# Sending more transposes of a two-layer hybrid encoder through transposing transfers

## The chip, the cores and the metric

The kernel runs on one core of a Trainium2 chip. A core has engines that each work through their own instructions in order: TensorE (PE, with its weight load PEld), VectorE (DVE), ScalarE (ACT), GpSimd (POOL) and SyncE (SP), which here issues almost all transfers (DMA). They wait for one another through semaphores. The metric is the device time of one execution in microseconds (us).

## The reference

Two layers over 256 tokens of 1024 channels, one sequence. What the change touches, cut to its core:

```python
u = rms_norm(h, g_mix_pre)
(gq, gk, gv, gg, ra_f, ra_b, aq, ak, av, gate_a, gate_b) = jnp.split(u @ w_in, offsets, axis=-1)
...
o_gla = rms_norm(o_f + o_b, g_gla_out)             # gated linear attention, two directions
branch_a = (o_gla * jax.nn.silu(gg)) @ w_o_gla     # the gated output
q = apply_axial_rope(rms_norm(aq, g_q_norm), cos, sin)
branch_b = gqa_attention(q, k, v) @ w_o_attn       # 8 query heads, 2 groups of 4
mixed = sigmoid(gate_a) * branch_a + sigmoid(gate_b) * branch_b
h = h + rms_norm(mixed @ w_out, g_mix_post)
```

Then a SwiGLU FFN with 2816 hidden channels and a per-layer embedding follow, each with norms and a residual add. All is f32.

## The kernel before

**Products.** Each f32 operand is split into a high part (a cast to the fp32r type) and a low part (value minus high part). A product is three matmuls, high by high, high by low and low by high, of 128 x 128 stationary activations and 512 columns of weights. Since the contraction runs over partitions, activations are needed transposed: channels on partitions, tokens free.

**Weights.** Every weight comes once from HBM in units of 1 MB on SP's queue, into one of two `raw` tiles. ACT casts a unit to `wh` in two pieces of 128 x 1024, DVE subtracts it to `wl` in two (`split`, L134), and PE uses it. Both kinds have four tiles each, so a cast can begin only when PE has given an older unit back (`done`). For gate B and three pairs of FFN blocks (2, 6, 8) a seven-product scheme is used: there some raw units are borrowed ("lent") from the `wh` and `wl` tiles or from a big tile, and DVE adds and combines units of 128 x 2048 between the casts.

**Order.** PE's work stands in program order: the long products are written out, and smaller jobs (transposes, attention, gla) are `Task` generators that go on at ticks, two to each group of twelve matmuls. The numbers a task yields (`W`, `WAIT_MIX`, `WAIT_TURNED` = 9 and others) are ticks that it lets pass. The framework orders the other engines' instructions by priority; `tc.high_priority(AHEAD)` puts instructions forward and `tc.issue_after(x)` puts them behind `x` on the same engine.

**Two ways of transposing.** `transpose_in` has PE transpose four 128 x 128 blocks into PSUM (L449, the queries' at L1267); ACT casts the result out of PSUM and DVE subtracts. `turn_out` and `take_in` use a transfer instead: ACT copies the f32 words into two planes of 16 bits (L463 or L468), SP issues a DMA transpose of the two planes (L469), and later ACT joins the planes to f32 words again (L476), casts, and DVE subtracts. Before, only the FFN's hidden blocks go that way, nine a layer, each with a fresh `mid` tile; the last pair's go through PE.

**The places.** `out_gate` (stage `gg`, PE's part in stage `gate`) multiplies gla output and SiLU of the gate and has PE transpose the product, sixteen blocks a layer (`turn_in(gT, sg, hf, W["g"])`). `attend(g)` transposes the queries of four heads for each half of the tokens (`hf`), takes the softmax, transposes it, and multiplies by the values. `merge(1)` adds the two gated branches and has PE transpose the sum in blocks (j, hf) for the out projection. `turned` in the FFN sends a hidden block out and takes it in.

## Time and profile before

| what | value |
|---|---|
| median of 3 runs | 909.61 us (909.36 to 910.53) |
| profiled execution | 909.68 us |
| its span | 907.9 us |
| granted TensorE clock | 0.999 |
| PE, PEld, DVE, ACT, POOL busy | 99%, 84%, 87%, 68%, 12% |
| moved by DMA | 178.16 MB, 196 GB/s on the mean |

The profile is of one execution; about 1.8 us of its time lie around the span. A row of the timeline gives the start, the time, the engine, the line of the kernel, the operation, the tiles written and read, and the count; idle time ahead of it and what ended it stand in brackets. A tile's name has its stage: `0gate` is the gate stage of layer 0, `1ffnin` the FFN of layer 1, `at` attention, `gla` linear attention, `gg` the gla output gate. Matmuls overlap, so one is best priced by the distance of starts and not by its duration.

### The profile page before, as it was taken

How to read it: one execution, taken by the hardware profiler on the slowest of the kernel's cores; microseconds unless marked ns; L12 is line 12 of the kernel's file. 1: busy time of each engine (PE TensorE's matmuls, PEld its weight loads, DVE VectorE, ACT ScalarE, POOL GpSimd, SP SyncE). 2: the span in 40 equal slices, each digit the busy share in tenths (PEclk: the TensorE clock that was granted, in tenths of full speed). 3: DMA queues.
4: the chain of work that ended last, by engine and by line, in shares of the span. 5: the costliest groups of instructions: out<-in, count | busy, mean ns of one | idle time of the engine just before them, and what ended most of it. 6: DMA issues, size and time to landing. Idle time of an engine off the chain costs nothing.

```text
span 907.9 us, 12157 instructions
## 1 busy us (share of the span) xinstructions
PE 898.8 (99%) x4479; PEld 762.2 (84%) x4479; DVE 790.2 (87%) x1021; ACT 620.5 (68%) x1011; POOL 105.9 (12%) x157
## 2 busy tenths in 40 slices
PE   9999999999999999999999999999999999999997
PEld 8898888888888887887898888888888888888886
DVE  7999989987668999998779899799876799999984
ACT  7688677564467787756676687675644796958563
POOL 3700221300100000000254001110000000000001
PEclk9999999999999999999999999999999999999999
DMA  8663445657397594956576424455573966858461
GB/s 283 219 189 136 140 140 191 216 187 249 115 288 204 173 301 146 317 170 233 180 279 204 168 93 140 139 186 185 186 241 100 309 180 206 254 210 264 150 231 47
DMA packets 108519, 178.16 MB, mean 196 GB/s; under 512 B 22494, under 2 KB 46566, under 8 KB 107948
## 3 DMA queue, kind: packets, MB, share of 16 engines
q1 hardware_dynamic: 108300, 177.25, 59.9%
q8 instruction: 35, 0.57, 0.3%
q14 instruction: 24, 0.20, 0.1%
q10 hardware_dynamic: 160, 0.14, 0.0%
HBM read 169.50 MB, written 3.15 MB: 190 GB/s over the span
## 4 chain that ended last, share of the span: by engine, by line
PE 78%; DVE 11%; DMA 4%; issue 4%; ACT 2%; POOL 0%; SPq 0%; POOLq 0%; ACTq 0%; DVEq 0%
PE acc_1ffnin L122 12%; PE acc_0gate L122 7%; PE acc_1gate L122 7%; PE acc_1ffnin L106 7%; DVE wl_0ffnin L134 6%; PE acc_1rq L122 3%; PE acc_0gqk L106 2%; PE acc_1gqk L106 2%; PE acc_1wout L122 2%; PE acc_0ple L122 2%; PE acc_1v L122 2%; PE acc_0gg L122 2%; PE acc_1gg L122 2%; PE acc_0v L122 2%; PE acc_0merge L122 2%
## 5 line engine op out<-in xcount | busy, mean ns | idle before, releaser
L134 ACT CAST wh_0ffnin<-raw_0ffnin 128x1024 fp32r<-128x1024 f32 x38 | 38.1, 1048 | 19.8 <-DMA raw_0ffnin<-in_w_ffn_out_dram 10.2
L134 ACT CAST wh_1ffnin<-raw_1ffnin 128x1024 fp32r<-128x1024 f32 x38 | 38.3, 1048 | 17.4 <-DMA raw_1ffnin<-in_w_ffn_out_dram 5.0
L134 DVE TENSOR_TENSOR wl_0ffnin<-raw_0ffnin,wh_0ffnin 128x1024 fp32r<-128x1024 f32 x38 | 44.6, 1219 | 5.8 <-ACT wh_0ffnin L134 5.8
L134 DVE TENSOR_TENSOR wl_1ffnin<-raw_1ffnin,wh_1ffnin 128x1024 fp32r<-128x1024 f32 x38 | 44.8, 1219 | 5.0 <-ACT wh_1ffnin L134 4.9
L106 PE MATMUL acc_0ffnin<-wh_0ffnin,big_0ffnin 128*128 128x512 f32 x176 | 45.4, 392 | 0.0
L106 PE MATMUL acc_1ffnin<-wh_1ffnin,big_1ffnin 128*128 128x512 f32 x176 | 45.1, 390 | 0.0
L122 PE MATMUL acc_0ffnin<-wh_0ffnin,big_0wout 128*128 128x512 f32 x168 | 41.8, 390 | 0.0
L122 PE MATMUL acc_1ffnin<-wh_1ffnin,big_1wout 128*128 128x512 f32 x168 | 41.5, 389 | 0.0
L106 PEld LDWEIGHTS acc_0ffnin<-wh_0ffnin,big_0ffnin 128*128 128x128 f32 x176 | 32.8, 188 | 7.5 <-DVE big_0ffnin L134 0.5
L106 PEld LDWEIGHTS acc_1ffnin<-wh_1ffnin,big_1ffnin 128*128 128x128 f32 x176 | 33.0, 188 | 6.9
L122 PEld LDWEIGHTS acc_0ffnin<-wh_0ffnin,big_0wout 128*128 128x128 f32 x168 | 31.4, 188 | 7.1 <-ACT wh_0ffnin L134 0.4
L122 PEld LDWEIGHTS acc_1ffnin<-wh_1ffnin,big_1wout 128*128 128x128 f32 x168 | 31.5, 188 | 6.5
L134 DVE TENSOR_TENSOR wl_1ffnin<-lent_1ffnin,wh_1ffnin 128x1024 fp32r<-128x1024 f32 x30 | 35.7, 1217 | 0.6 <-ACT wh_1ffnin L134 0.6
L134 DVE TENSOR_TENSOR wl_0ffnin<-lent_0ffnin,wh_0ffnin 128x1024 fp32r<-128x1024 f32 x30 | 35.6, 1216 | 0.1
L134 ACT CAST wh_1ffnin<-lent_1ffnin 128x1024 fp32r<-128x1024 f32 x30 | 30.7, 1051 | 5.4 <-PE acc_1ffnin L106 3.9
L134 ACT CAST wh_0ffnin<-lent_0ffnin 128x1024 fp32r<-128x1024 f32 x30 | 30.4, 1053 | 3.6 <-DVE lent_0ffnin L332 3.4
L134 ACT CAST wh_0gate<-raw_0gate 128x1024 fp32r<-128x1024 f32 x20 | 19.9, 1049 | 14.4 <-DMA raw_0gate<-in_w_o_attn_dram 6.1
L134 ACT CAST wh_1gate<-raw_1gate 128x1024 fp32r<-128x1024 f32 x20 | 19.9, 1048 | 13.9 <-PE acc_1gate L122 5.9
L134 DVE TENSOR_TENSOR wl_0gate<-raw_0gate,wh_0gate 128x1024 fp32r<-128x1024 f32 x20 | 24.2, 1257 | 5.2 <-ACT wh_0gate L134 5.1
L134 DVE TENSOR_TENSOR wl_1gate<-raw_1gate,wh_1gate 128x1024 fp32r<-128x1024 f32 x20 | 23.5, 1221 | 5.1 <-ACT wh_1gate L134 5.1
L106 PE MATMUL acc_0ffnin<-wl_0ffnin,big_0ffnin 128*128 128x512 f32 x88 | 24.6, 394 | 0.6 <-DVE wl_0ffnin L134 0.6
L106 PE MATMUL acc_1ffnin<-wl_1ffnin,big_1ffnin 128*128 128x512 f32 x88 | 24.0, 391 | 0.0
(730 smaller groups left out, 2731.7 us busy)
## 6 DMA issues: line engine op xcount, KB each, us to landing
raw_0ffnin<-in_w_ffn_out_dram SPq DMA_DIRECT2D x11, 1024.0 KB, 5.9
raw_1ffnin<-in_w_ffn_out_dram SPq DMA_DIRECT2D x11, 1024.0 KB, 5.5
lent_0ffnin<-in_w_ffn_in_dram SPq DMA_DIRECT2D x6, 1024.0 KB
lent_1ffnin<-in_w_ffn_in_dram SPq DMA_DIRECT2D x6, 1024.0 KB, 7.5
raw_0v<-in_w_in_dram SPq DMA_DIRECT2D x4, 1024.0 KB, 5.8
raw_0gate<-in_w_o_gla_dram SPq DMA_DIRECT2D x4, 1024.0 KB, 6.8
raw_0gate<-in_w_o_attn_dram SPq DMA_DIRECT2D x4, 1024.0 KB, 5.2
raw_0wout<-in_w_ffn_in_dram SPq DMA_DIRECT2D x8, 512.0 KB, 4.6
```

Source lines behind the costliest of these rows:

```text
L106: return nc.tensor.matmul(o, lhsT, rhs, start=start, stop=stop)
L122: nc.tensor.matmul(o, x, y, start=start and n == 0, stop=stop and n == len(seq) - 1, **kw)
L134: return nc.scalar.copy(hi, src), nc.vector.tensor_tensor(out=lo, in0=src, in1=hi.bitcast(F32), op=ALU.subtract)
```

## The change

- Gated output: no PE transposes. Each half tile of 512 channels of `sg` is sent out by `turn_out`, in place: its planes go to the part of `gg` that has been used, the transpose comes back into `sg`. It is taken in after 9 ticks (hf = 0) or 11 (hf = 1), the second half tile a tick later. Four transfers a layer in place of sixteen transposes.
- Queries of g = 1: sent out after the last exponential of g = 0, with the planes over g = 0's half of the same tile, and taken in where PE transposed before. Two transfers a layer in place of eight transposes.
- Mix: the one block with j < hf, that is j = 0 and hf = 1, is sent out when it is made and taken in after 9 ticks, behind the last addition of the merge. One transfer a layer in place of four transposes.
- FFN: the transpose now comes back into the hidden block's own tile and the join goes to the planes' tile, so a `mid` tile serves two blocks.
- Queue order: the stream notes its last load (SP) and last weight cast (ACT and DVE). A transfer is issued behind that load, and a join with its cast and subtraction behind that weight cast (`turn`).

In all 56 PE transposes go; 14 transfers come, each with a split and a join on ACT. PE's order is otherwise the same but for a few matmuls that change places around the second group's scores. DVE has the same kinds of subtraction.

```diff
@@ -28,9 +28,10 @@
 WAIT_NEXT, WAIT_IN, WAIT_H = (7, 9), ((6, 9), (6, 6)), ((3, 5), (3, 5))
-WAIT_MIX = 3, 6
+WAIT_MIX = 3, 6, 9
 WAIT_SPREAD = 12
-W = dict(r=5, z=6, s0=4, s=3, s1=9, o0=1, o=1, k=4, q=3, a0=1, a1=4, a2=4, a3=1, g=6)
+W = dict(r=5, z=6, s0=4, s=3, s1=9, o0=1, o=1, k=4, q=3, a0=1, a1=4, a2=4, a3=1)
+WAIT_GATED = 9, 11
 
@@ -256,6 +257,7 @@
             self.loads, self.jobs, self.lend, self.last = [], [], False, {}
+            self.queue = {}
             pairs = {}
@@ -294,7 +296,9 @@
                     if self.open:
-                        nc.sync.dma_start(dst, src)
+                        load = nc.sync.dma_start(dst, src)
+                        if not x.own:
+                            self.queue["SP"] = load
                     else:
@@ -317,7 +321,7 @@
             for piece in self.put(x):
-                split(*piece)
+                self.queue["ACT"], self.queue["DVE"] = split(*piece)
 
@@ -348,9 +352,16 @@
                 for piece in pieces or ():
-                    self.last[n] = split(*piece)
+                    self.last[n] = self.queue["ACT"], self.queue["DVE"] = split(*piece)
                 if pieces:
                     self.load()
+
+        def turn(self, *engines):
+            stack = ExitStack()
+            for e in engines:
+                if e in self.queue:
+                    stack.enter_context(tc.issue_after(self.queue[e].ins))
+            return stack
 
@@ -452,32 +463,29 @@
 
-    def turn_out(src, k, hf):
+    def turn_out(src, parts, mixed=False):
 
         with tc.high_priority(AHEAD):
-            both, turned = halves(mid())
-            turned = turned.bitcast(U16)
-            parts = both.bitcast(U16).rearrange("p (s c) -> p s c", s=2)
-            words = src.bitcast(U16)
-            if hf is None:
+            planes, words = (t.bitcast(U16) for t in (parts, src))
+            if mixed:
                 nc.scalar.copy(
-                    parts.rearrange("p s (k h f) -> p s k h f", k=2, f=P),
+                    planes.rearrange("p (s k h f) -> p s k h f", s=2, k=2, f=P),
                     words.rearrange("p (h k f s) -> p s k h f", h=2, f=P, s=2),
                 )
             else:
-                nc.scalar.copy(parts, words.rearrange("p (c s) -> p s c", s=2))
-            nc.sync.dma_start_transpose(out=turned.rearrange("p (x t) -> p x t", t=P), in_=parts.rearrange("p s c -> p (s c)"))
-        return both, turned
-
-    def take_in(sp, both, turned, k, hf):
-
-        n, tn = (2, T) if hf is None else (4, P)
-        hi, lo = sp.at(k, n, (hf or 0) * P, tn)
-        nc.scalar.copy(
-            both.bitcast(U16).rearrange("p (k t s) -> p k t s", s=2, t=tn),
-            turned.rearrange("p (s k t) -> p k t s", s=2, t=tn),
-        )
-        split(hi, lo, both.rearrange("p (k t) -> p k t", t=tn))
+                nc.scalar.copy(planes.rearrange("p (s c) -> p s c", s=2), words.rearrange("p (c s) -> p s c", s=2))
+        with ws.turn("SP"):
+            nc.sync.dma_start_transpose(out=words.rearrange("p (x t) -> p x t", t=P), in_=planes)
+
+    def take_in(hi, lo, src, parts):
+
+        tn = hi.shape[-1]
+        with ws.turn("ACT", "DVE"):
+            nc.scalar.copy(
+                parts.bitcast(U16).rearrange("p (k t s) -> p k t s", s=2, t=tn),
+                src.bitcast(U16).rearrange("p (s k t) -> p k t s", s=2, t=tn),
+            )
+            split(hi, lo, parts.rearrange("p (k t) -> p k t", t=tn))
 
@@ -1261,12 +1269,14 @@
                 yield W["q"]
-                ps = aux()
-                for i in range(4):
-                    hd = 4 * g + i
-                    nc.tensor.transpose(ps[:, i * P : (i + 1) * P], qrs[hf][:, hd * P : (hd + 1) * P], ident)
                 qh, ql = halves(mid(F32R))
-                split(qh, ql, ps)
+                if g == 0:
+                    ps = aux()
+                    for i in range(4):
+                        nc.tensor.transpose(ps[:, i * P : (i + 1) * P], qrs[hf][:, i * P : (i + 1) * P], ident)
+                    split(qh, ql, ps)
+                else:
+                    take_in(*(t.rearrange("p (i t) -> p i t", t=P) for t in (qh, ql)), *halves(qrs[hf])[::-1])
                 qs.append((qh, ql, qss[hf][:, 4 * g : 4 * g + 4]))
@@ -1274,6 +1284,10 @@
                 yield W["a1"]
+            if g == 0:
+                for qr in qrs:
+                    with tc.issue_after(last_exp[0].ins):
+                        turn_out(*halves(qr)[::-1])
             for hf in range(2):
@@ -1459,7 +1473,16 @@
                     vmul(t, t, on[:, hf, s])
-                turn_in(gT, sg, hf, W["g"])
+                xs = [(t, gg[:, hf, j * 512 : (j + 1) * 512]) for j, t in enumerate(halves(sg))]
+                for x in xs:
+                    turn_out(*x)
+
+                def turn(hf=hf, xs=xs):
+                    for j, x in enumerate(xs):
+                        yield WAIT_GATED[hf] if j == 0 else 1
+                        take_in(*gT.at(4 * j, 4, hf * P, P), *x)
+
+                gT.makers[hf].append(Task(turn(), part[0]))
 
@@ -1512,16 +1535,24 @@
 
+        mixed = []
+
         def merge(br):
             def then(j, hf, o):
                 sl = [s[:, hf, j * 512 : (j + 1) * 512] for s in sgate[: br + 1]]
                 vmul(sl[br], o, sl[br])
                 if br == 1:
-                    nc.vector.tensor_tensor(out=sl[0], in0=sl[0], in1=sl[1], op=ALU.add)
+                    mixed.append(nc.vector.tensor_tensor(out=sl[0], in0=sl[0], in1=sl[1], op=ALU.add))
 
                     def turn():
-                        yield WAIT_MIX[hf]
-                        transpose_in(mixT, sl[0], 4 * j, 4, hf)
+                        if j < hf:
+                            turn_out(*sl)
+                        yield WAIT_MIX[2 if j < hf else hf]
+                        if j < hf:
+                            with tc.issue_after(mixed[-1].ins):
+                                take_in(*mixT.at(4 * j, 4, hf * P, P), *sl)
+                        else:
+                            transpose_in(mixT, sl[0], 4 * j, 4, hf)
 
@@ -1567,7 +1598,7 @@
         part[0] = f"{l}ffnin"
-        hid = Split()
+        hid, spare = Split(), []
         us = [[ws.take() for _ in range(2)] for _ in range(2)]
@@ -1577,9 +1608,12 @@
                 else:
-                    x = turn_out(src, k, hf)
+                    if not spare:
+                        spare.extend(halves(mid()))
+                    parts = spare.pop()
+                    turn_out(src, parts, hf is None)
                     yield WAIT_TURNED
-                    take_in(hid, *x, k, hf)
+                    take_in(*(hid.at(k, 2, 0, T) if hf is None else hid.at(k, 4, hf * P, P)), src, parts)
 
```

How it moves ACT in the gate stage of layer 0, before (`lent`, `raw` and a big tile hold weights; `aux_0gg` is PE's transpose in PSUM):

```order
L134 CAST wh_0gate_1680<-lent_0gate_1670 128x1024 x2
L134 CAST wh_0gate_1747<-raw_0gate_1676 128x1024 x2
L134 CAST big_0gg_1719<-aux_0gg_1714 128x4x128
L134 CAST big_0gg_1727<-aux_0gg_1722 128x4x128
L134 CAST big_0gg_1719<-aux_0gg_1730 128x4x128
L134 CAST big_0gg_1727<-aux_0gg_1737 128x4x128
L1475 ACTIVATE big_0gate_1744<-acc_0gate_1598,rs_start_120 128x512
L1475 ACTIVATE big_0gate_1744<-acc_0gate_1599,rs_start_121 128x512
L134 CAST wh_0gate_1781<-big_0gate_1672 128x1024 x2
L134 CAST wh_0gate_1805<-raw_0gate_1678 128x1024
L740 COPY mid_0gate_1788<-acc_0gate_1790 128x512
```

and after:

```order
L476 COPY big_0gg_1272<-mid_0gg_1632 128x1024 x2
L135 CAST wh_0gate_1684<-lent_0gate_1674 128x1024
L476 COPY big_0gg_1272<-mid_0gg_1642 128x1024 x2
L135 CAST wh_0gate_1684<-lent_0gate_1674 128x1024
L1498 ACTIVATE big_0gate_1718<-acc_0gate_1594,rs_start_120 128x512
L1498 ACTIVATE big_0gate_1718<-acc_0gate_1595,rs_start_121 128x512
L135 CAST wh_0gate_1721<-raw_0gate_1680 128x1024 x2
L484 COPY big_0gg_1272<-mid_0gg_1632 128x1024 x2
L135 CAST big_0gg_1749<-big_0gg_1272 128x4x128
L135 CAST big_0gg_1759<-big_0gg_1272 128x4x128
L135 CAST wh_0gate_1763<-big_0gate_1676 128x1024 x2
L484 COPY big_0gg_1272<-mid_0gg_1642 128x1024 x2
```

Four casts out of PSUM stood together behind the casts of two units. Now four splits (L476, two to a row) surround the first unit's pieces, and the joins (L484, two to a row) with their casts stand between the next units' casts; the second pair's casts follow.

ACT at the splits of the second group's queries in layer 0, before (`mx`, `sm` belong to the softmax of g = 0, `aux_0at` is its transpose):

```order
L1237 ACTIVATE mid_0at_811,sm_0at_822<-aux_0at_812,mx_0at_819,qss_0rq_164 128x256 x2
L1302 ACTIVATE big_0gqk_639<-acc_0gqk_783 128x256
L1237 ACTIVATE mid_0at_811,sm_0at_838<-aux_0at_828,mx_0at_835,qss_0rq_164 128x256 x2
L134 CAST wh_0gqk_911<-raw_0gqk_773 128x1024
L134 CAST mid_0at_892<-aux_0at_887 128x512
L134 CAST mid_0at_900<-aux_0at_895 128x512
L134 CAST wh_0gqk_911<-raw_0gqk_773 128x1024
```

and after:

```order
L1245 ACTIVATE mid_0at_811,sm_0at_822<-aux_0at_812,mx_0at_819,qss_0rq_164 128x256 x2
L1316 ACTIVATE big_0gqk_639<-acc_0gqk_783 128x256
L1245 ACTIVATE mid_0at_811,sm_0at_838<-aux_0at_828,mx_0at_835,qss_0rq_164 128x256 x2
L476 COPY mid_0rq_161<-mid_0rq_161 128x1024
L476 COPY mid_0rq_163<-mid_0rq_163 128x1024
L135 CAST mid_0at_896<-aux_0at_891 128x512
L135 CAST mid_0at_904<-aux_0at_899 128x512
L135 CAST wh_0gqk_915<-raw_0gqk_773 128x1024 x2
```

Two copies have come in behind the last exponential, ahead of the casts of the transposed softmax and of weights.

ACT at the first hidden blocks of the FFN in layer 0, before (L1596 is the SiLU, L468 the split, L476 the join):

```order
L1596 ACTIVATE t_0ffnin_2594<-acc_0ffnin_2622 128x256
L453 COPY mid_0wout_2298<-aux_0wout_2643 128x512
L468 COPY mid_0ffnin_2665<-t_0ffnin_2594 128x1024
L476 COPY mid_0ffnin_2665<-mid_0ffnin_2665 128x1024
L1596 ACTIVATE t_0ffnin_2668<-acc_0ffnin_2669 128x256
L134 CAST wh_0ffnin_2702<-raw_0wout_2522 128x1024 x2
```

and after (the SiLU is L1630, the split L476, the join L484):

```order
L476 COPY mid_0ffnin_2651<-t_0ffnin_2580 128x1024
L1630 ACTIVATE t_0ffnin_2654<-acc_0ffnin_2655 128x256
L135 CAST wh_0ffnin_2688<-raw_0wout_2508 128x1024 x2
L135 CAST mid_0ffnin_2715<-mid_0wout_2280 128x512
L135 CAST mid_0ffnin_2724<-mid_0wout_2281 128x512
L135 CAST mid_0ffnin_2733<-mid_0wout_2281 128x512
L135 CAST wh_0ffnin_2740<-raw_0emb_2575 128x1024 x2
L1630 ACTIVATE t_0ffnin_2654<-acc_0ffnin_2697 128x256
L135 CAST wh_0ffnin_2749<-lent_0ffnin_2682 128x1024 x2
L476 COPY mid_0ffnin_2651<-t_0ffnin_2654 128x1024
L484 COPY mid_0ffnin_2651<-t_0ffnin_2580 128x1024
L135 CAST mid_0ffnin_2769<-t_0ffnin_2704 128x512
```

The join stood right behind its split; now it comes nine rows later, after the second block's SiLU, three units' casts and the second split.

## The prediction

> **What bounds the kernel now.** I read the busy shares first, then the chain that ended last, then what PE and its weight load wait for.
>
> ```profile
> PE 898.8 (99%) x4479; PEld 762.2 (84%) x4479; DVE 790.2 (87%) x1021; ACT 620.5 (68%) x1011; POOL 105.9 (12%) x157
> PE 78%; DVE 11%; DMA 4%; issue 4%; ACT 2%; POOL 0%; SPq 0%; POOLq 0%; ACTq 0%; DVEq 0%
> ```
>
> PE is busy for 898.8 of 907.9 us, so its work is the time, and taking work from it pays as long as the engines that feed it keep up. DVE, with 87%, is the next. The waits of the weight load (waited for, total us, times, longest) say how near it is already:
>
> ```profile
> PEld acc_0ffnin L106 <- DVE wl_0ffnin L134: 1.5, 2, 0.8
> PEld acc_0ffnin L122 <- DVE wl_0ffnin L134: 0.7, 1, 0.7
> PEld acc_0ffnin L122 <- ACT wh_0emb L134: 0.5, 1, 0.5
> PEld acc_0ffnin L122 <- ACT wh_0ffnin L134: 0.4, 1, 0.4
> ```
>
> The largest are these, and every wait on weights is in layer 0's FFN. Elsewhere DVE and ACT deliver in time, though by how much differs from stage to stage, and the change is costed stage by stage.
>
> **What leaves PE.** PE's rows around the gated output's sixteen transposes:
>
> ```profile
> 147.70 1.91 PE L449 MATMUL aux_0gg<-ident,mid_0gg 128*128 128x128 f32 x16
> 149.36 2.08 PE L122 MATMUL acc_0gate<-wh_0gg,big_start 128*128 128x512 f32 x8
> 151.28 0.39 PE L122 MATMUL acc_0gate<-wl_0gg,big_start 128*128 128x512 f32 x1
> ```
>
> PE's rows at an undisturbed place of the same stage:
>
> ```profile
> 166.70 1.07 PE L122 MATMUL acc_0gate<-wh_0gate,big_0gg 128*128 128x512 f32 x4
> 167.60 1.07 PE L122 MATMUL acc_0gate<-wl_0gate,big_0gg 128*128 128x512 f32 x4
> ```
>
> And around the four transposes of a query block:
>
> ```profile
> 97.22 0.60 PE L1267 MATMUL aux_0at<-ident,mid_0rq 128*128 128x128 f32 x4
> 97.57 0.48 PE L122 MATMUL acc_0v<-wh_0v,big_start 128*128 128x512 f32 x1
> ```
>
> Sixteen transposes hold PE from 147.70 to 149.36, 1.66 us. The eight matmuls behind them take 1.92 where 0.90 for four would make 1.80, so 0.12 goes on top: 1.78 us. A group of four takes 0.35 and the same 0.12, 0.47 us. A layer loses sixteen for the gated output, two groups of four for the queries (g = 1) and one for the mix: 1.78 + 3 x 0.47 = 3.19 us, 6.4 us for both. The program order has no PE work added. That is the whole direct gain.
>
> **What comes in its place.** A transposing transfer already serves the FFN, and its parts are these: the split, the join, and on SP the issue (ns least, median, most) and the time to landing.
>
> ```profile
> L468 ACT COPY mid_0ffnin<-t_0ffnin 128x1024 uint16<-128x1024 uint16 x6 | 6.3, 1044 | 0.8 <-DVE t_0ffnin L127 0.8
> L476 ACT COPY mid_0ffnin<-mid_0ffnin 128x1024 uint16<-128x1024 uint16 x9 | 10.5, 1177 | 12.0 <-DMA mid_0ffnin<-mid_0ffnin 12.0
> L469 SPq DMA_TRANSPOSE mid_0ffnin<-mid_0ffnin x9: 1237/1250/1922, 268.3 to 377.1; - x9
> DMA to landing us min/median/max: 3.3/4.8/6.2
> ```
>
> ACT pays 1.04 for the split and 1.18 for the join: 2.22 us for each of 14 transfers, 31.1 us. SP issues 14 times 1.25, 17.5 us. ACT's casts and DVE's subtractions keep their number and size; they read SBUF in place of PSUM, which I cost at nothing. Data arrives 3.3 to 6.2 us after the issue. None of this is PE's, so it costs what it makes late.
>
> At this place the Trainium skill speaks against the change: "VectorE: DVE Perf Modes", in its rules for kernel authors and the section on the three transpose paths, says to use TensorE for a 128 by 128 transpose where a PSUM destination will do, and gives 1309 ns for such a block by DMA against 390 ns on TensorE. One transfer here holds eight 16-bit blocks, so by that page I estimate 8 x 1.309 = 10.5 us for each and 42 us for the gate's four in a row; the sum would then be a loss of tens of us. The trace does not agree: eight blocks land in 3.3 to 6.2 us, and TensorE takes 0.47 for four.
>
> **Gate stage, twice.** ACT's waits from 143.4 to 168:
>
> ```profile
> ACT wh_0gate L134 <- PE acc_0gate L122: 5.5, 4, 2.1
> ACT big_0gate L1475 <- PE acc_0gate L122: 1.1, 1, 1.1
> ACT wh_0gate L134 <- DMA lent_0gate<-in_w_in_dram: 0.5, 1, 0.5
> ```
>
> The stage by windows (us, then PE, PEld, DVE, ACT, POOL busy, PE's clock, DMA share, GB/s):
>
> ```profile
> 140.00:150.00 10.00, 10.00 (x54) 8.55 (x53) 10.00 (x17) 7.94 (x12) 0.00 (x0) 1.00 0.89 327
> 150.00:160.00 10.00, 10.00 (x46) 8.26 (x45) 10.00 (x12) 6.59 (x9) 0.00 (x0) 1.00 0.00 0
> 160.00:170.00 10.00, 10.00 (x46) 8.28 (x45) 10.00 (x9) 5.75 (x7) 0.00 (x0) 1.00 0.65 204
> ```
>
> The subtraction that makes the low half of w_o_gla's first unit, and SP's loads of that weight:
>
> ```profile
> 163.33 2.35 DVE L134 TENSOR_TENSOR wl_0gate<-raw_0gate,wh_0gate 128x1024 fp32r<-128x1024 f32 x2
> 142.01 0.37 SPq L297 DMA_DIRECT2D raw_0gate<-in_w_o_gla_dram  x1
> 159.00 0.37 SPq L297 DMA_DIRECT2D raw_0gate<-in_w_o_gla_dram  x1
> ```
>
> Four transfers add 4 x 2.22 = 8.9 us to ACT, which idles 7.1 there: 1.8 too much, and PE comes 1.8 sooner, so ACT's casts are up to 3.6 us late at the stage's end. DVE has nothing free to catch up with. Its low half of the weights is done at 165.68, and PE takes it at 167.60, a slack of 1.9 us. So PE waits at most 1.7 us a layer. The least is nothing: the idle is ACT waiting for PE to give back weight tiles, and a later cast there may still be soon enough. The rows don't prefer either end; I take the middle, 0.9, so 1.8 for both layers. On SP the four issues (5 us) now stand ahead of the first load of w_o_gla. It went out at 142.01; now it follows the last split, which cannot start much before 147.70, where PE began to transpose the same tile, so it goes out about 10 us later, by 152. Between 142.5 and 159.00 no other weight load is held up. The joins wait 9 and 11 ticks, and with a tick each six matmuls (1.35 us) that is 12 us and more, twice the 6.2 of one transfer; what queues behind a join if four in a row need longer is the cast of the next weights, a rival below.
>
> **Queries (g = 1).** The two splits stand on ACT behind the last exponential of g = 0, ahead of the gla decays' logarithms, on which DVE waits.
>
> ```profile
> 60.00:70.00 10.00, 10.00 (x69) 9.16 (x68) 9.85 (x25) 9.31 (x23) 0.00 (x0) 1.00 0.61 190
> 70.00:80.00 10.00, 10.00 (x50) 8.35 (x49) 9.31 (x16) 9.11 (x20) 0.00 (x0) 1.00 0.38 130
> 80.00:90.00 10.00, 10.00 (x54) 8.56 (x53) 10.00 (x15) 7.90 (x16) 0.00 (x0) 1.00 0.31 105
> 90.00:100.00 10.00, 10.00 (x59) 8.66 (x58) 10.00 (x18) 7.71 (x17) 5.61 (x4) 1.00 0.22 67
> ```
>
> The second group's first query on DVE and then on PE:
>
> ```profile
> 98.46 0.68 DVE L134 TENSOR_TENSOR mid_0at<-aux_0at,mid_0at 128x512 fp32r<-128x512 f32 x1
> 99.04 0.65 PE L106 MATMUL aux_0at<-big_0kv,mid_0at 128*128 128x256 f32 x4
> ```
>
> And layer 1 at the place of the splits:
>
> ```profile
> 526.00:536.00 10.00, 10.00 (x51) 8.39 (x50) 9.03 (x12) 8.47 (x19) 0.00 (x0) 1.00 0.20 79
> ```
>
> Both splits, 2.1 us, push a DVE that has 0.15 + 0.69 = 0.84 us free before 80 and nothing until 100: it is 1.25 us late by then. The query's low half ends at 99.14 while PE's scores with it have begun at 99.04, so there is no slack. PE waits between nothing (if other DVE work is overtaken) and 1.25 + 0.94, the last being the two groups by which PE is early: 2.2 us. I take DVE's own lateness, 1.3. In layer 1 DVE has 0.97 free at the same place; 2.1 - 0.97 = 1.1 is the upper end, nothing the lower, and ACT has 1.53 free in the same window, so I lean down: 0.4. Together 1.7, which eats the two layers' 1.9 for queries almost whole.
>
> **Mix.** One block a layer, 2.22 us on ACT, 9 ticks for the transfer, used late in the out projection; no wait of PE or its weight load stands in that stage above, so I cost it at nothing; if that cover is gone, it gives back its 0.47 a layer.
>
> **FFN's joins behind the weight casts.** ACT before goes straight from a split to its join and waits for the transfer:
>
> ```profile
> 274.00 1.17 ACT L476 COPY mid_0ffnin<-mid_0ffnin 128x1024 uint16<-128x1024 uint16 x1 [5.76 <-DMA mid_0ffnin<-mid_0ffnin]
> 275.48 0.43 DVE L127 TENSOR_TENSOR t_0ffnin<-acc_0ffnin,t_0ffnin 128x256 f32<-128x256 f32 x1 [6.25 <-ACT t_0ffnin L1596]
> 290.00:300.00 10.00, 9.74 (x42) 7.30 (x41) 10.00 (x11) 9.76 (x13) 0.00 (x0) 1.00 0.19 36
> ```
>
> ACT stands for 5.76 us; the SiLU behind it is late, so DVE stands for 6.25; then DVE is full, and PE drops to 9.74 of 10 between 290 and 300. With the join nine rows later that idle is filled. Of the waits quoted first (3.1 us on the weight load, part of it covered by the matmuls in flight) I take back 1.1: those at this place (0.7 and 0.4), and no more, since the one on wh_0emb comes ahead of any join and the others follow loads. The ends are 2.5 back, if all go, and 2 lost, if a join or a transfer that now stands behind a load comes late: the hidden blocks then hold the out steps up. Layer 1 shows no wait of PE, so there is nothing to win.
>
> **Sum.** -6.4 - 1.1 + 1.8 + 1.7 = -4.0 us. Against the profiled execution (909.68, of which the span is 907.9) that is 905.7; the median of the runs, 909.61, is as good as the same.
>
> **Rivals.**
> 1. Everything that was pushed stays hidden: both paybacks zero, the FFN's gain whole. 6.4 and 1.1 to 2.5 give 900.8 to 902.2. For it speaks that PE waited nowhere outside the FFN; against it DVE's full windows in just the stages that lose the transposes.
> 2. The gain is eaten: the stages are held by DVE, not PE, at 10.00 in each window of the gate and of the queries. Then PE's 6.4 turn into waits at the next weights or scores, the gates keep none, and the time is about 909. Against it: slack of 1.9 at the gate covers the whole 1.78.
> 3. Slower: a gate join reached before its transfer has landed. It is the wait of 274.00 again, at a worse place: behind it on ACT stand the casts of w_in's and w_o_gla's units, DVE has no idle to make up, and the slack of 1.9 is used by PE's own advance. Each us that ACT waits there is a us for PE, in both layers. At 4 us (below the 5.76 seen) the gate pays 2 x 4 in place of 1.8: -4.0 - 1.8 + 8 = +2.2, 911.9. It is slower than before from 2.9 us of wait on, by 0.2% from 3.8. Four transfers in a row behind DMA engines that are 0.89 busy are for it; the 12 us of ticks and the empty DMA of 150 to 160 are against it. It is also where a page's rule against DMA transposes would end (the Trainium skill, "VectorE: DVE Perf Modes", rules for kernel authors), on the durations of this trace.
>
> **How the numbers follow.** The forecast, 903 to 907.7, has 0.47; rival 1 0.15; rival 2 0.2; rival 3 0.18. Within 0.2% (1.8 us, about what this measurement can tell) is rival 2. The range goes from close to rival 1's better end to close to rival 3's time, 901.2 to 911.6, which leaves out about half of each; for the forecast alone it is 903 to 907.7. Faster 0.62, same 0.2, slower 0.18.
>
> **What would show it.** PE's transposes gone at 147 to 149, the gate stage shorter by about 1 us, a new short wait of PE or its weight load on wl_0gate or wl_1gate; a wait on the second group's queries near 99; the 12.0 us of ACT's waits at joins in layer 0's FFN mostly gone, and with them DVE's 6.25. I am wrong if ACT waits for transfers in the gate stage (rival 3), if PE's waits add up to 6 us (rival 2) or if none is new (rival 1).

## The result and the profile after

| | median | range, runs | profiled execution (span) |
|---|---|---|---|
| before | 910.07 us | 908.86 to 913.42, 6 | 909.68 (907.9) |
| changed | 916.44 us | 914.23 to 919.33, 6 | 916.64 (914.8) |

The changed kernel is slower, by a ratio of 1.0067 (1.0043 to 1.009). I had said 905.7, and 911.6 at most.

Busy times and chain of the changed kernel:

```profile
PE 898.1 (98%) x4423; PEld 758.1 (83%) x4423; DVE 792.7 (87%) x1021; ACT 646.3 (71%) x1039; POOL 107.8 (12%) x157
...
PE 56%; DVE 19%; ACT 12%; DMA 7%; issue 4%; POOL 1%; POOLq 0%; SPq 0%; ACTq 0%; DVEq 0%
```

PE lost 56 transposes and yet is busy for as long as before (898.1 against 898.8), a first sign that some of its work ran slower. ACT's share of the chain went from 2% to 12%. What PE waited for, in the changed kernel (total us, times, longest):

```profile
PE acc_0wout L123 <- ACT big_0merge L135: 3.0, 1, 3.0
PE acc_1wout L123 <- ACT big_1merge L135: 2.8, 1, 2.8
...
PE acc_1v L123 <- DVE mid_1at L135: 0.7, 1, 0.7
PE acc_1ffnin L123 <- ACT wh_1ffnin L135: 0.5, 1, 0.5
PE acc_0ffnin L123 <- ACT wh_0ffnin L135: 0.4, 1, 0.4
...
PE aux_0at L107 <- DVE mid_0at L135: 0.4, 1, 0.4
```

The two long waits are at the out projection, for the mix block (`big_0merge`, `big_1merge`). That is the part I had costed at nothing.

To see where the 6.9 us of span come from, take the start of each stage's first matmul in both timelines and see by how much the difference grows:

| stage of PE | layer 0 | layer 1 |
|---|---|---|
| up to the gla products | +0.6 | -0.1 |
| from there to the gate stage (queries) | +0.3 | +0.2 |
| gate stage | -1.8 | -1.8 |
| to the out projection (mix transposes gone) | -0.5 | -0.5 |
| out projection | +6.3 | +3.1 |
| FFN | -0.9 | +1.9 |
| rest | 0.0 | +0.1 |

The first row's 0.6 arises before 31 us, ahead of anything that the change moves, so it belongs to the execution; in the other kernels' traces below the same stretch is 0.1 to 1.1 us longer than before. The FFN's rows hold such a share too, as the part on the FFN's order shows.

The gate stage's rows, from its first matmul to that of the next stage, before:

```profile
135.42 0.86 PE L122 MATMUL acc_0gate<-wh_0gg,big_start 128*128 128x512 f32 x3
...
201.15 0.62 PE L122 MATMUL acc_0merge<-wh_0gate,big_0at 128*128 128x512 f32 x2
```

and in the changed kernel:

```profile
136.37 0.86 PE L123 MATMUL acc_0gate<-wh_0gg,big_start 128*128 128x512 f32 x3
...
200.32 0.84 PE L123 MATMUL acc_0merge<-wh_0gate,big_0at 128*128 128x512 f32 x3
```

65.73 us became 63.95: the whole 1.78 us, without a wait of PE. And this although ACT is full there, with 1.5 us of idle where 7.1 had been (windows, columns as in the prediction):

```profile
150.00:160.00 10.00, 10.00 (x46) 8.28 (x45) 9.97 (x11) 10.00 (x13) 0.00 (x0) 1.00 0.91 197
160.00:170.00 10.00, 10.00 (x46) 8.29 (x45) 9.76 (x9) 10.00 (x14) 0.00 (x0) 1.00 0.43 152
```

```profile
ACT big_0gg L476 <- DVE mid_0gg L128: 1.5, 1, 1.5
```

Now the out projection of layer 0 in the changed kernel: SP, ACT and PE.

```profile
220.14 1.25 SPq L478 DMA_TRANSPOSE big_0gate<-big_0gate  x1
222.84 0.37 SPq L299 DMA_DIRECT2D raw_0merge<-in_w_out_dram  x1
...
220.50 1.05 ACT L135 CAST wh_0merge<-raw_0gate 128x1024 fp32r<-128x1024 f32 x1
...
228.19 1.99 ACT L135 CAST wh_0merge<-raw_0merge 128x1024 fp32r<-128x1024 f32 x2 [4.09 <-DMA raw_0merge<-in_w_out_dram]
230.09 1.16 ACT L484 COPY big_0gate<-big_0gate 128x1024 uint16<-128x1024 uint16 x1
231.28 0.62 ACT L135 CAST big_0merge<-big_0gate 128x512 fp32r<-128x512 f32 x1
...
228.31 1.09 PE L123 MATMUL acc_0wout<-wl_0merge,big_0merge 128*128 128x512 f32 x4
232.44 0.79 PE L123 MATMUL acc_0wout<-wh_0merge,big_0merge 128*128 128x512 f32 x1 [3.04 <-ACT big_0merge L135]
```

The join (L484, 230.09) doesn't wait for its transfer, which was issued at 220.14. It stands on ACT behind the cast of the last unit of w_out, and that cast waits 4.09 us for a load issued at 222.84. The same load and cast before:

```profile
215.46 5.00 SPq L297 DMA_DIRECT2D raw_0merge<-in_w_out_dram  x2
...
222.61 0.57 ACT L134 CAST big_0merge<-aux_0merge 128x512 fp32r<-128x512 f32 x1
225.08 2.00 ACT L134 CAST wh_0merge<-raw_0merge 128x1024 fp32r<-128x1024 f32 x2 [1.90 <-DMA raw_0merge<-in_w_out_dram]
```

There the second load went out at 215.46 + 5.00 - 0.37 = 220.09, 2.75 us earlier, though PE was later, and the weight cast ended 3.1 us sooner. The mix block's own cast stood ahead of it (222.61), out of PSUM and without a wait.

Behind the wait PE's clock is halved (windows of the changed kernel: us, PE busy, granted clock, DMA share, GB/s):

```profile
231.00:232.00 1.00, 0.00 (x0) 0.67 0.00 0
232.00:233.00 1.00, 0.56 (x1) 0.50 0.17 27
...
237.00:238.00 1.00, 1.00 (x5) 0.50 0.00 0
238.00:239.00 1.00, 1.00 (x7) 0.91 0.00 0
```

From 232.4 to 237.7 twelve matmuls start 0.43 us apart in place of 0.23 (232.44 to 237.72 is 5.28 us, twelve at full clock are 2.7): 2.6 us more. Wait and slow clock are 5.6 of the 6.3. In layer 1, after a wait of 2.8 us, the clock stayed at 1.00.

### The profile page after: what moved, and what is told of

It reads as the page before. It is cut to its first block, busy times and chain, and to the rows that moved or that the text cites. A ratio compares the mean times of both kernels' runs of the same rounds, so it can differ in the third digit from the quotient of the medians.

```text
span 914.8 us, 12065 instructions
## 1 busy us (share of the span) xinstructions
PE 898.1 (98%) x4423; PEld 758.1 (83%) x4423; DVE 792.7 (87%) x1021; ACT 646.3 (71%) x1039; POOL 107.8 (12%) x157
## 4 chain that ended last, share of the span: by engine, by line
PE 56%; DVE 19%; ACT 12%; DMA 7%; issue 4%; POOL 1%; POOLq 0%; SPq 0%; ACTq 0%; DVEq 0%
PE acc_1ffnin L123 9%; PE acc_0ffnin L123 8%; PE acc_1ffnin L107 5%; DVE wl_0gate L135 3%; DVE wl_1gate L135 3%; PE acc_1rq L123 3%; PE acc_0ffnin L107 3%; PE acc_1v L123 2%; PE acc_0ple L123 2%; DVE wl_0ffnin L135 2%; PE acc_0wout L123 2%; PE acc_1ple L123 2%; PE acc_1gg L123 2%; PE acc_0gqk L107 2%; PE acc_1wout L123 2%
```

## The experiments

All ratios are to the kernel before, run on the same chip at the same time. "By PE" means that a part's old code is back; where only some parts are put in, the FFN stages of a kernel whose FFN is the old one show the instructions of the kernel before in the same order on PE, DVE, ACT and SP, so the parts can be put in one by one. Times are medians of 4 to 10 executions; a trace is of one of them.

**The mix block by PE again, and its join alone moved.** The first edit puts the old task back:

```diff
-                        if j < hf:
-                            turn_out(*sl)
-                        yield WAIT_MIX[2 if j < hf else hf]
-                        if j < hf:
-                            with tc.issue_after(mixed[-1].ins):
-                                take_in(*mixT.at(4 * j, 4, hf * P, P), *sl)
-                        else:
-                            transpose_in(mixT, sl[0], 4 * j, 4, hf)
+                        yield WAIT_MIX[hf]
+                        transpose_in(mixT, sl[0], 4 * j, 4, hf)
```

> The changed kernel with the mix block (j = 0, hf = 1) transposed by PE again. Theory A (the mix transfer alone is what costs: PE waits 3.0 and 2.8 us for its cast, and in layer 0 runs 5.3 us at half clock behind that): the steps of +5.95 and +3.06 us at the out projection go and 0.47 a layer comes back, so the span is about 914.8 - 9.0 + 0.9 = 906.7 us, the time about 908.5, a ratio of 0.998 to the kernel before. Theory B (the weight stream is late there for other reasons and PE would wait for something else instead, a weight or another mix block): a wait of 2 us or more a layer remains at the out projection, 911 to 914 us.

Measured: 909.68 us, 1.0000 (0.999 to 1.0011), span 907.8. Both waits are gone and the span fell by 7.0 us, as much as the whole loss against the kernel before (6.9). Theory A's span of 906.7 was 1.1 too low, about what layer 1's FFN is longer by than in the changed kernel (1.35). No wait of 2 us took the place, so theory B falls. The longest that PE has left behind the kernel's start is this one (total us, times, longest):

```profile
PE aux_1wout L460 <- DVE mid_1wout L552: 0.7, 1, 0.7
```

The second edit leaves the transfer and takes only the join's place:

```diff
-                            with tc.issue_after(mixed[-1].ins):
-                                take_in(*mixT.at(4 * j, 4, hf * P, P), *sl)
+                            take_in(*mixT.at(4 * j, 4, hf * P, P), *sl, free=True)
...
-        with ws.turn("ACT", "DVE"):
+        with nullcontext() if free else ws.turn("ACT", "DVE"):
```

> The changed kernel with one order less: the join of the mix block needn't follow the last weight cast; on ACT it now stands ahead of the last unit of w_out (its two casts) instead of behind it, and nothing else moves. Theory A1 (the join waits for the weight cast ahead of it, which waits 4.1 us for its load): PE's waits at the out projection (3.0 and 2.8 us and the slow clock) vanish, about 907.5 us. Theory A2 (the transfer itself or its split is what is late, whatever stands ahead of the join): ACT waits for the transfer at the join, PE still waits 2 us or more a layer, above 912 us.

Measured: 910.48 us, 1.0015 (1.0003 to 1.0027), span 907.0. ACT in this kernel:

```profile
223.24 1.16 ACT L484 COPY big_0gate<-big_0gate 128x1024 uint16<-128x1024 uint16 x1
224.43 0.62 ACT L135 CAST big_0merge<-big_0gate 128x512 fp32r<-128x512 f32 x1
227.40 2.00 ACT L135 CAST wh_0merge<-raw_0merge 128x1024 fp32r<-128x1024 f32 x2 [2.35 <-DMA raw_0merge<-in_w_out_dram]
```

and what PE still waits for:

```profile
PE acc_1wout L123 <- ACT big_1merge L135: 0.8, 1, 0.8
PE acc_0wout L123 <- ACT big_0merge L135: 0.8, 1, 0.8
```

The join ran at 223.24 without any wait for its transfer, 6.9 us earlier than in the changed kernel. Theory A1 holds in the main, though it said that the waits would vanish: the late thing is the cast ahead of the join, and A2's wait for the transfer isn't there. The 0.8 us that stay are the other mix block's cast, which also stands behind the weight cast (its row in this trace begins at 229.30). The median is 3 us above my 907.5, the profiled execution (908.88) 1.4, so this run shows the cause but doesn't regain everything.

**The gated output by PE again.**

```diff
-                xs = [(t, gg[:, hf, j * 512 : (j + 1) * 512]) for j, t in enumerate(halves(sg))]
...
-                gT.makers[hf].append(Task(turn(), part[0]))
+                turn_in(gT, sg, hf, 6)
```

> The changed kernel with the gated output transposed by PE again (sixteen transposes a layer). The gate stage gains 1.78 us a layer in the changed kernel, so on its own this is 3.6 us slower. Theory B1 (ACT's added work in the gate stage makes the stream of weights late, by 2.5 us against PE at the out projection, and that is what makes the mix join late): with the stream early again PE's waits at the out projection fall from 3 us to below 1, and the slow clock goes: 916.4 + 3.6 - 8 = about 912. Theory A (the order of the join alone): the waits stay within 1 us of what they are, about 919 to 920.

Measured: 915.62 us, 1.0057 (1.0038 to 1.0076), span 915.7. PE's waits for the mix block in this kernel:

```profile
PE acc_0wout L123 <- ACT big_0merge L135: 1.0, 1, 1.0
...
PE acc_1wout L123 <- ACT big_1merge L135: 0.3, 1, 0.3
```

The waits fell from 3.0 and 2.8 to 1.0 and 0.3 and the slow clock is gone, as B1 said, though no instruction around the mix was touched. The time is 3.6 us above B1's 912, and 3.4 below theory A's 919. In the profiled execution, the slowest of five, layer 1's FFN is 4.4 us longer than before; whether that is this edit's doing is not shown.

**The queries by PE again.**

> The changed kernel with the second group's queries transposed by PE again. From the two traces the query stages lost 0.31 us in layer 0 and 0.22 in layer 1 against the kernel before, where the transposes alone should have given 0.94 each: this run should be 0.5 us faster than the changed kernel (about 916), with PE's waits on mid_0at and mid_1at (0.4 and 0.7) gone. Rival: the splits' lateness is not confined to the query stage but carries through the weight stream to the out projection, then the waits of 3.0 and 2.8 there shrink as well and it is 2 us or more faster.

Measured: 920.63 us, 1.0118 (1.0101 to 1.0134). Slower, not faster; both expectations missed. The trace shows the waits for the mix block little changed (2.6 and 2.3), but now with the slow clock in both layers, and layer 1's FFN 5.5 us longer. Why it is slower is not shown. What the queries cost must be read from a kernel without the mix transfer.

**One part alone on the kernel before, and two together.**

> The kernel before with nothing but the mix transfer (gated output and queries by PE, the FFN's turns as before). Theory B1 (the mix join is late only because the gate stage's joins made the weight stream late against PE, as the fall of PE's waits from 3.0 and 2.8 to 1.0 and 0.3 with the gated output by PE says): waits of about 1.0 and 0.3 against two times 0.47 of transposes, so 910.1, no difference that can be told. Theory A (the order of the join alone is enough): the 5.5 and 2.6 us net come back, about 917.

> The kernel before with nothing but the gated output by transfer. The gate stage gave 1.78 us a layer without a wait of PE. Theory F: it keeps that, 909.7 - 3.6 = 906.1. Rival G (the stream sets the time of the stages behind, PE's lead is given back there): above 908, with PE's waits of 1 to 3 us in the out projection or the FFN.

> The kernel before with two of the change's parts: the gated output and the mix block by transfer (queries by PE, the FFN's turns as before). Alone the first gave -3.4 us, the second +1.7 in the profile and +4 in the times. Theory C (the two meet at the out projection: the gate's joins make the stream late against PE, the mix join stands behind that stream's casts): PE's waits for the mix block grow from 1.1 and 1.8 to 2.5 to 3 us a layer, the slow clock comes in layer 0, and the time is 911 to 914. Rival: they add, waits stay below 2, 907 to 910.

> The kernel before with nothing but the second group's queries by transfer. Theory: as in the changed kernel's trace, the stages from the first gla products to the gate stage lose 0.3 us in layer 0 and 0.2 in layer 1 by waits of PE on mid_0at and mid_1at, and nothing follows: 909.7 + 0.5 = 910.2, the same. Rival: the waits there are harmless and the 1.9 us of transposes are won: 907.8.

> The kernel before with the gated output and the queries by transfer, mix and FFN as before. Theory: 906.3 + 0.5 = 906.8, between the gated output alone and 907.5. Rival (the two latenesses meet as gate and mix may): above 908.5, with PE waiting for weights in the gate stage or behind it.

| parts by transfer | median | ratio (interval) | span |
|---|---|---|---|
| mix alone | 913.68 | 1.0039 (1.0025 to 1.0053) | 909.6 |
| gated output alone | **906.26** | **0.9969 (0.9956 to 0.9982)** | 904.4 |
| gated output and mix | 916.29 | 1.0066 (1.0044 to 1.0088) | 912.0 |
| queries alone | 911.05 | 1.0008 (0.9993 to 1.0022) | 911.1 |
| gated output and queries | 908.40 | 0.9988 (0.9977 to 1.0) | 906.4 |

Waits for the mix block with the mix transfer alone:

```profile
PE acc_1wout L123 <- ACT big_1merge L135: 1.8, 1, 1.8
PE acc_0wout L123 <- ACT big_0merge L135: 1.1, 1, 1.1
```

and with the gated output as well:

```profile
PE acc_0wout L123 <- ACT big_0merge L135: 2.7, 1, 2.7
PE acc_1wout L123 <- ACT big_1merge L135: 2.3, 1, 2.3
```

The gated output alone is faster than both kernels, and its 906.26 is close to the 906.1 that 2 x 1.78 us give. That the two agree so well is partly luck. In its trace the gate stage gives 1.78 us in layer 1 but 1.18 in layer 0, where PE waits for a cast of weights:

```profile
PE acc_0gate L123 <- ACT wh_0gate L135: 0.2, 1, 0.2
```

This wait and the slower matmuls around it are 0.6 us, ACT's lateness that the prediction had priced. Layer 0's out projection is 1.05 us longer as well, and the two FFNs, with the old code, are together 2.2 shorter.

The mix transfer alone costs 4 us in the times, between theory B1 (910.1) and theory A (917), and 1.7 in the profiled execution; its ten runs lie between 910.9 and 915.7, so an execution with the slow clock and one without may both be among them, which I can't tell from the times. With the gated output in, it costs 9.6 us: each kernel against its own runs of the kernel before, -3.5 becomes +6.1. As a sum of parts 910.2 would have come out, where 916.29 did, as slow as the whole change. So the order of the join costs by itself, and the gated output's transfer makes it cost more (theory C: its waits and its slow clock came, its 911 to 914 holds the profiled execution, 913.78, and not the median). The queries bring nothing alone; with the gated output they make it 2 us slower, a little under the 908.5 of the rival and above the theory's 907.5. The meeting point can be read as the lead of w_out's last load over PE's first matmul of the out projection in layer 0:

| kernel | last load of w_out | PE's first | lead | PE's wait |
|---|---|---|---|---|
| before (no mix transfer) | 220.09 | 223.87 | 3.8 | 0 |
| gated output alone (no mix transfer) | 222.77 | 223.59 | 0.8 | 0 |
| mix alone | 222.11 | 223.90 | 1.8 | 1.1 |
| gated output by PE | 222.97 | 224.82 | 1.9 | 1.0 |
| gated output and mix | 222.97 | 222.33 | -0.6 | 2.7 |
| changed | 222.84 | 222.55 | -0.3 | 3.0 |
| changed, join first | 222.25 | 221.99 | -0.3 | 0.8 |

With the join behind the cast, lead and wait sum to 2.1 to 2.9. The mix's own split takes about 2 us of lead: it and another block's cast now stand between the two casts of one unit, and the load waits for DVE's subtraction of the second piece, whose buffer it takes. The gated output takes another 2.4: PE comes 1.6 us sooner (0.4 of it because that execution began faster, which moves the load as well) and the load 0.9 later. The last row has the same lead, and little wait, because its join isn't in that queue; nor does the short lead of the gated output alone make PE wait for the mix block, which PE transposes there.

**The FFN's order.** First alone, then with the gated output in layer 0 only. A caution first: in the five kernels of the table of parts, whose FFN is the old one, layer 0's FFN is 0.1 to 3.1 us shorter than in the trace before and layer 1's 0.0 to 1.7 longer. A difference of that size in one trace is therefore not the new order's.

> The kernel before with nothing but the FFN's new order (transfers behind loads, joins behind weight casts, in place). In the run with the mix block by PE, PE gained 1.5 us in layer 0's FFN and lost 3.2 in layer 1's against the kernel before. Theory F (the new order does that by itself): about 909.7 - 1.5 + 3.2 = 911.4, within 1. Rival G (layer 1's loss comes from PE being 3.5 us early there, so that it meets a stream that is no faster): layer 1 loses at most what layer 0 brought, 908 to 909.7.

> The gated output by transfer and the FFN's new order in layer 0 only; queries and mix by PE, layer 1's FFN as before. Theory F: -3.6 and -1.5, 904.6, the best of all. Rival G: no better than the gated output alone, 906 to 908.5.

Measured: the FFN's order alone 912.83, 1.0035 (1.0023 to 1.0047); with the gated output and in layer 0 only 908.48, 0.9987 (0.9974 to 1.0001), which is 2.2 us behind the gated output alone. In the first, layer 0's FFN gains 0.75 us and layer 1's loses 2.8; theory F's 911.4 within 1 holds the profiled execution, 911.80, and misses the median by 0.4. PE waits in layer 1 for casts of weights, 1.9 us that the kernel before doesn't have:

```profile
PE acc_1ffnin L107 <- ACT wh_1ffnin L135: 1.2, 1, 1.2
PE acc_1ffnin L123 <- ACT wh_1ffnin L135: 0.7, 1, 0.7
```

In the second rival G's figure came out: the order in layer 0 adds nothing to the gated output. Then its parts, in place without order, and with one of the two orders each:

```diff
-        with ws.turn("SP"):
+        with tc.high_priority(AHEAD):
...
-        with ws.turn("ACT", "DVE"):
+        with nullcontext():
```

> The kernel before with the FFN's transfers in place and the planes' tile shared by two blocks, but without the queue order (no transfer behind a load, no join behind a weight cast; 68 lines of ACT's and 64 of SP's order in the FFN differ from the kernel before, mostly where a join names another tile). Theory F1 (the queue order costs the 2 to 3 us of the FFN's part): back to 909.7 within 0.8. Rival F2 (the tiles do: a hidden block's tile is held until its join, so a SiLU behind it waits): 911.5 to 913 as with the order.

> The kernel before with the FFN's transfers in place and issued behind the stream's loads, but the joins where they may go (not behind the weight casts). The new order alone lost 2.0 us in the profile and 0.35% in the times, in place without any order 1.1 us and 0.13%. Theory J (the joins behind the casts cost: ACT then meets loads of w_ffn_out that haven't landed, 16.8 us of such waits in layer 1 against 5.0 before): this run is as the one in place only, 910.9 within 0.8, with under 11 us of ACT's waits on those loads in layer 1. Theory S (the transfers behind loads cost): 912 to 913.

> The counterpart: in place, the joins behind the weight casts, the transfers where they may go on SP's queue. Theory J: 912 to 913, with ACT's waits on loads of w_ffn_out in layer 1 at 15 us or more. Theory S: 910.9 within 0.8.

Measured: in place only 910.88, 1.0013 (0.9999 to 1.0027); transfers behind loads 913.93, 1.0032 (1.0013 to 1.0052); joins behind casts 912.79, 1.0025 (1.001 to 1.0039). The run in place is 0.4 us outside F1's bound and well below F2, so the order is likely the larger part, though the intervals of 1.0013 and 1.0035 overlap.

Which order it is stays open. J and S each come near in the run that keeps their own order and fail on the other. Even there J's sign is missing (ACT waits 9.9 us on the loads of w_ffn_out in layer 1, where J said 15 or more), and S's 912 to 913 is passed by 0.9. Each order alone has a median of about 2.4 (joins) and 3.5 us (transfers) above the kernel before, with intervals that overlap that of the run in place.

One more thing moves. "The change" says that PE's order is otherwise the same, but with the joins behind the casts matmuls of the FFN change places on PE too, from about 341 us on in layer 0 and 790 on in layer 1; the whole order moves more of them than the joins alone. In place, or with only the transfers behind loads, PE's order is the old one. What this costs is not shown.

ACT's waits show what they did. Before:

```profile
ACT wh_0ffnin L134 <- DMA raw_0ffnin<-in_w_ffn_out_dram: 10.2, 3, 5.3
...
ACT wh_1ffnin L134 <- DMA raw_1ffnin<-in_w_ffn_out_dram: 5.0, 2, 4.2
ACT mid_1ffnin L476 <- DMA mid_1ffnin<-mid_1ffnin: 3.2, 3, 1.7
```

In the kernel with the FFN's order alone:

```profile
ACT wh_0ffnin L135 <- DMA raw_0ffnin<-in_w_ffn_out_dram: 18.1, 5, 6.2
...
ACT wh_1ffnin L135 <- DMA raw_1ffnin<-in_w_ffn_out_dram: 16.8, 5, 7.5
```

and with the transfers behind loads alone:

```profile
ACT mid_0ffnin L484 <- DMA t_0ffnin<-mid_0ffnin: 14.1, 5, 6.2
ACT wh_0ffnin L135 <- DMA raw_0ffnin<-in_w_ffn_out_dram: 10.6, 3, 5.4
```

ACT's 12.0 us at the joins of layer 0 are gone, but 8 us more stand before casts whose load hasn't landed; in layer 1, 3.2 went and 12 came. With the transfers behind loads and the joins free, the joins wait longer (14.1). The wait moved from one kind of transfer to the other.

## Why the prediction was wrong, step by step

- **Direct gain, 6.4 us.** Sizes right: 1.78 a layer at the gates, 0.47 to 0.49 ahead of the out projection. At the queries it didn't show, see below.
- **Gate stage, 1.8 us back.** In the changed kernel nothing came back there. ACT did fill up as worked out (10.00 of 10), but the wait for weight tiles had enough room, the lower end of my bounds. With the queries by PE 0.4 to 0.7 us does come back, in layer 0 only. What I missed is that the lateness doesn't end with the stage: PE keeps its 1.78 us, the stream's loads stay or come later, and the slack is used up for whatever comes next.
- **Mix, "I cost it at nothing": the step that failed.** Its cover was given as "no wait of PE or its weight load stands in that stage". That is a fact of a profile in which the loads of w_out had a lead of 3.8 us. I named neither what stands ahead of the join on ACT, a cast that before already waited 1.90 us for its load, nor the split's place between two casts of one unit. In the changed kernel the part pays 6.3 and 3.1 us. I allowed it 0.47 a layer if the cover went, when a lost cover costs the wait and not the transposes. The step accounts for 7.4 of the 10.4 us between forecast and result: with the mix by PE, the sum without this part is -4.0 + 0.94 = -3.1, and the kernel shows -0.1.
- **Queries, 1.7 us back.** Layer 0: 0.94 of transposes and +0.3 in the timeline, 1.25 back, as sized (1.3). Layer 1: 0.94 and +0.2, about 1.2 back where I took 0.4; the wait is PE's on `mid_1at`, 0.7 us. Alone the part is 1.0008, no gain. With other parts in, taking it out made the kernel about 4 us slower (changed kernel) or 2 faster (with the gated output); that is not explained.
- **FFN, -1.1.** The second step that failed, and large enough for the other 3 us: -1.1 was forecast, and alone the part measures +3.1. In layer 0 this trace shows -0.9, near the forecast, but the old FFN shows -0.1 to -3.1 in other traces, so the agreement may be luck. "Layer 1 shows no wait of PE, so there is nothing to win" forgot that there was something to lose: +1.9, and +2.8 with the order alone. With the order alone ACT's waits moved to the loads, and PE waits 1.9 us for the casts behind them.
- **Rival 2** (the gain eaten by waits of PE, about 909) had its sign come true, waits that add up to 6 us: 5.8 at the out projection alone. But it placed them at the gates and the queries, with DVE as the cause, and the gates kept their whole gain.
- **Rival 3** (slower, by a join in ACT's queue with casts around it) came nearest, in kind. Its place and its wait were wrong: not in the gate stage, not for the transfer, but behind a weight cast. The rule on transposes that the prediction takes from the Trainium skill ("VectorE: DVE Perf Modes", rules for kernel authors) is to use TensorE where a PSUM destination will do. It wasn't the reason for the loss: the gated output alone, sixteen transposes a layer by DMA, is faster, 0.9969.
- **The slow clock** was in no step: 2.6 us behind one wait.

The parts alone sum to -3.5 (gate) + 4.0 (mix) + 0.9 (queries) + 3.1 (FFN) = +4.5 us in the times, the whole change is +6.4. What is left over isn't assigned: gate and mix together are alone 5.6 above their sum, and queries and FFN then add nothing. Layer 1's FFN, 1.7 to 5.5 us longer wherever the whole new order is in and 0.0 to 1.7 where the FFN is the old one, is not explained beyond ACT's waits on the loads of w_ffn_out and PE's behind them.

## What to carry to other kernels

"Hidden" is a statement about a queue, not about an engine's idle share: before a join or a copy is costed at nothing, write down the instruction ahead of it on its engine, what that one waits for, and by how much it led in the old trace. Time taken from the bounding engine moves its consumers earlier while the loads stay, so each gain shortens the lead of every later stage; price the later parts with the leads that the earlier ones leave. When a change has several parts, measure each alone: here one part was worth 3.5 us and the rest hid it.

## What was not expected of the hardware

- A wait of 3.04 us of PE left it at half clock for 5.3 us, 2.6 us more. Waits of 2.69 us (gated output and mix, layer 0), 2.58 and 2.28 (queries by PE, both layers) also did, but there the clock fell only 1.2 to 1.4 us after PE had started again; a wait of 2.77 us in layer 1 of the changed kernel did not, nor one of 2.33 (gated output and mix, layer 1). The length alone doesn't decide it. The Trainium skill, "TensorE: Matmul & The Clock Gate", in Part 1 on the clock gate, has PE fall to half rate after an idle window of about 3.4 us and calls the window free-running. The halving agrees with the trace (0.50). The waits do not: each of the four that led to it is shorter than such a window, and by the page's rule none of them would. From the granted clock of the windows I estimate that the half rate lasted 3.4 us after the three shorter of them and 6.8 after the longest, one and two of the page's windows. Whether a wait's place in such a window decides is a guess that no run here tests.
- Four transposing transfers in a row were issued within 5.45 us in the gate stage of layer 0, and ACT waited for none of them. SP in the changed kernel:

```profile
146.44 5.45 SPq L478 DMA_TRANSPOSE mid_0gg<-big_0gg  x4
```
